# A 16x512x1024 tanh-gated double matmul: the first row tile of x loaded in one transfer

## The chip, the cores and the metric

The kernel runs on one NeuronCore of a Trainium2 chip. Five engines work side by side, each through its own list of instructions in order: TensorE (PE in the profile; its weight loads are listed as PEld), VectorE (DVE), ScalarE (ACT), GpSimd (POOL) and SyncE (SP). SP and ACT start plain DMA transfers, POOL starts DMA transfers that convert float32 to float16 on the way. The metric is the device time of one launch in microseconds; three runs of the kernel before took 296.96, 297.32 and 301.93 us, so the median is 297.32 us.

## The reference

```python
batch, m, k, n = 16, 512, 1024, 768
x: (16, 512, 1024) float32;  w1, w2: (1024, 768) float32

y1 = np.matmul(x, w1)
y2 = np.matmul(x, w2)
return (np.tanh(y1) * y2).astype(np.float32)
```

With batch and rows taken together, x has 8192 rows: 64 row tiles of 128 rows. One row tile is 128x1024 float32, 512 KB; its half along k (512 columns) is 256 KB.

## The kernel before, in words

**Tiling.** The columns of both weight matrices are cut into three blocks: `a` (the first 512 columns of w1), `b` (the first 512 of w2) and `g` (the last 256 of w1 beside the last 256 of w2). Along k there are eight slices of 128. The first four row tiles (0 to 3, `HEAD`) are multiplied plainly: per tile and block eight matmuls of 128x512 are summed in one PSUM bank (line 430), then ACT takes the tanh and DVE multiplies. The other 60 row tiles go in 20 triples. A triple would need 18 products of half a row tile's depth, and is worked out from 15 products (line 457, four matmuls each) of sums of x halves (made by DVE, line 421) and sums of weight blocks (line 412), which ACT and DVE add up (lines 461 and 467), before the tanh (470) and the last multiplication (475).

**Order.** `Planner` orders all the work while the program is built. It knows each operation's cost, what it needs, and when a transfer lands (the table `lands`, and `LANDING` for the transposed tiles), and it writes one order per engine; the 15 products of each triple follow in a fixed order from a start time, `START`. No loop is left at run time. The plan decides which engine does the work where two can, the order on each engine, and the PSUM bank.

**How a row tile gets into place.** Plain matmuls need x transposed in float16. For tiles 0 to 3, SP loads float32 halves: `x00` is tile 0, half 0, `x01` is tile 0, half 1, and so on. Halves `x00` and `x10` are transposed on PE in float32 (`FP32`), the other halves are first converted by DVE (`cx..`, line 368) and then transposed on PE in float16 (`PT..`, line 380). ACT or DVE copies the transposed half from PSUM to SBUF (`e..`, line 366). Only then can the matmuls with that half run.

**Queues at the start.** SP starts its transfers in the order of `on_sp`: first x00, x10, x20, x30, then x01, x60, x11, a4, a5, and so on. ACT starts a0 to a3, the first four k slices of block a, at the same time. The semaphores of these transfers go round a ring of eight, so that SP's fifth transfer waits until one of the first eight has landed, the sixth waits for the next, and so on. The twelve transfers of POOL (block b, and the tiles 4, 5 and the second half of 6) wait behind a small copy that reads a converted g slice (line 504).

**Constant matmuls.** Before any data is there, PE runs the matmuls of `WARM` on a tile of constants, seven of 512 columns into banks 0 to 6 (line 337); their results are not used. After the transposes of x00, and again after those of x10, stands one `FILL`: three more of them, 512, 512 and 256 columns. In the plan the first FILL is free to start after `PT00` and the second after `PT10`.

The calls of the head in the order of the plan before: WARM, PT00, FILL, the first matmul of tile 0 (named m0a0 below: tile, block, k slice), PT10, FILL, m0a1, m1a0, m1a1, PT20, m0a2, m1a2, m2a0, PT30 and so on.

Of the kernel before, what the change touches and what calls it, by code (L numbers as in the profile page):

```python
# [226 lines left out]
def kernel(  # L227
# [21 lines left out]
    XT_BUFS, XH_BUFS, S_BUFS, O_BUFS, C_BUFS = 12, 8, 2, 9, 2  # L249
    WARM = 512, 512, 512, 512, 512, 512, 512  # L250
    FILL = 512, 512, 256
    FREE = 3
    TURNS = (2, 0, 1), (0, 2, 1)
    LANDING = {7: 35.9, 9: 37.2, 8: 39.4, 10: 47.4, 11: 48.3, 12: 49.2, 13: 55.0, 14: 56.3, 15: 57.6}
    rows = list(range(HEAD)) + [HEAD + 3 * i + r for i in range(TRIPLES) for r in (TURNS[i] if i < len(TURNS) else (0, 1, 2))]
# [87 lines left out]
    def x_staged(mt, h):  # L343
        return x_first[mt][:, half(h)] if mt < HEAD else arena[:, STAGED * F:(STAGED + 1) * F]

    def load_first(e, mt, h):
        pin(nc.sync.dma_start(x_staged(mt, h), xf[mt][:, half(h)]))

# [160 lines left out]
    FINE = (5, 36, 37, 45)  # L509
    START = 28.6  # L510
    P7 = 13.0
    ORIGIN = START - 6 * SLOT

# [15 lines left out]
    LAG_FROM, LAG = 21.5, 1.2  # L529
    on_sp = "x00 x10 x20 x30 x01 x60 x11 a4 a5 x21 a6 x31 a7".split() + [f"g{k}{t}" for k in range(KH) for t in range(2)]  # L530
    by_pool = "b0 b4 b1 b5 x61 x4 b2 x51 x50 b6 b3 b7".split()
    GATES = {"b0": ("cg0", w_cols("g", 0)[:, :1])}
    arrivals = on_sp[4:] + by_pool
    size = {"x": 0.68, "a": 0.68, "g": 0.75, "b": 0.63}
    lands = dict(zip("x00 a0 x10 a1 x20 a2 x30 a3".split(), (4.31, 4.47, 6.13, 6.53, 7.7, 8.17, 9.05, 9.44)))
    now = 9.2
    for n in arrivals:
        now += 1.25 if n in by_pool and n[0] == "x" and len(n) == 2 else size[n[0]]
        lands[n] = now + (LAG if now > LAG_FROM else 0.0)

    for k in range(4):
        op(f"La{k}", {"act": 0.45}, -100, [], load_w, "a", k, issued=[f"La{k - 1}"] if k else [], lands=lands[f"a{k}"])
    for n, what in enumerate(on_sp):
        before = [f"L{on_sp[n - 1]}"] if n else []
        if what[0] == "x":
            op(f"L{what}", {"sp": 0.05}, 0.1 * n - 100, [], load_first, int(what[1]), int(what[2]), issued=before, lands=lands[what])
        else:
# [44 lines left out]

    for n, after in enumerate(("PT00", "PT10")):
        op(f"f{n}warm", {"pe": 0.54}, -50, [after], fill, ("f", n), chains=[("f", n)])
    for mt in range(HEAD):
        for h in range(2):
            if (mt, h) not in FP32:
                op(f"cx{mt}{h}", {"dve": 0.37}, lands[f"x{mt}{h}"] - 1, [f"Lx{mt}{h}"], cast_x, mt, h)
            by_pe(mt, h, lands[f"x{mt}{h}"] - 2, f"Lx{mt}{h}" if (mt, h) in FP32 else f"cx{mt}{h}")
        op(f"D{mt}", {"act": 1.05}, START + 8, [f"Lx{mt}0", f"Lx{mt}1"], abs_x, mt, hold=11 + 4 * mt)  # L600
    for mt in rows[HEAD:BY_PE]:
# [154 lines left out]
    for mt in range(MT):  # L756
        i = (mt - HEAD) // 3 if mt >= HEAD else -1
        if mt < HEAD:
            kept = mt == HEAD - 1
            for t in range(2 if mt == 1 else 0):  # L760
                op(f"st{mt}{'ag'[t]}", {"sp": 0.05}, 1e3, outs[mt][t:t + 1], store, mt, t * F, (F, G)[t], behind=[f"p12.{11 + 2 * mt}"], xfer=0.5)
            if mt != 1:
                op(f"st{mt}", {"sp": 0.05}, 1e3, outs[mt][:1] if kept else outs[mt], store, mt, F if kept else 0, G if kept else N, behind=[f"p12.{11 + 2 * mt}"], xfer=1.0)
            for t in range(2 if kept else 0):
                op(f"st{mt}{chr(88 + t)}", {"sp": 0.4, "act": 0.4}, 2e4, outs[mt][1 + t:2 + t], store, mt, t * G, G, xfer=0.4)
            continue
# [37 lines left out]
    for n, cols in enumerate(WARM):  # L804
        constants(banks[n], cols)
    for n in sorted(soon, key=lambda n: plan.start_of[n]):
# [109 lines left out]
```

## Time and profile before

| What | us |
|---|---|
| median of three runs | 297.32 |
| the profiled execution, whole | 297.16 |
| its span on the core, which the profile shows | 295.6 |
| PE busy | 289.5 |
| DVE busy | 255.8 |
| ACT busy | 224.4 |
| POOL busy | 42.3 |

The span begins with the first instruction of the kernel's body and ends with the last one; 1.56 us of the profiled execution lie outside it. "Busy" is the time in which at least one instruction of the engine runs; matmuls are pipelined, so that their starts tell more than their durations. In a row of the timeline the first number is the start in us from the span's start, the second the duration, then come engine, line, operation and tile, the count of instructions that the row merges, and in brackets the idle time before it with what ended it. In a row of the windows stand, for a stretch of time, each engine's busy time with its count of instructions, the granted clock of TensorE, the share of time in which the 16 DMA engines were busy, and the bytes that they moved in GB/s.

### The profile page before, as it was taken

To read this page: it belongs to the slowest core of one execution; us is meant where nothing else is said; L and a number is where in the kernel's file an instruction comes from. 1 tells how busy PE (TensorE), PEld (TensorE's weight loads), DVE (VectorE), ACT (ScalarE), POOL (GpSimd) and SP (SyncE) were. 2 spreads that over 40 slices of the span, in tenths; PEclk is the share of its full clock that TensorE was granted. 3 is DMA by queue.
4 is the path that set the end of the run, shared out by engine and by line. 5 is a ranking of instruction groups with operands and counts; after the bars stand their busy time and mean duration, and the time that the engine had idled before them with its cause. 6 is when DMAs were issued, how large, how long until landed. Compare 5 with 4: busy or idle time off the path is not lost. (4 is left out here: it accounts for less than half of the span.)

```text
span 295.6 us, 4588 instructions
## 1 busy us (share of the span) xinstructions
PE 289.5 (98%) x1374; PEld 132.3 (45%) x1374; DVE 255.8 (87%) x552; ACT 224.4 (76%) x454; POOL 42.3 (14%) x94
## 2 busy tenths in 40 slices
PE   7999999999999999999999999999999999999994
PEld 3445444444444444444444444444444444444442
DVE  1679999999989998898989888898988889898875
ACT  2698599799878878877888888677777767778442
POOL 0065022202102102202012021020211100000000
PEclk9999999999999999999999999999999999999999
DMA  6999999999999999989999999999999999241234
GB/s 217 391 321 204 182 141 169 210 247 230 240 194 197 247 226 216 252 218 239 204 190 246 231 236 270 164 271 264 224 298 225 213 175 324 104 162 53 109 136 169
DMA packets 84858, 63.63 MB, mean 215 GB/s; under 512 B 62816, under 2 KB 67168, under 8 KB 84832
## 3 DMA queue, kind: packets, MB, share of 16 engines
q1 hardware_dynamic: 73888, 45.10, 59.7%
q0 software_dynamic: 9936, 16.65, 36.0%
q10 hardware_dynamic: 1008, 1.57, 1.5%
q8 instruction: 11, 0.18, 0.2%
q14 instruction: 15, 0.12, 0.1%
HBM read 39.85 MB, written 25.17 MB: 220 GB/s over the span
## 5 line engine op out<-in xcount | busy, mean ns | idle before, releaser
L457 PE MATMUL bank<-b,early_x 128*128 128x512 f16 x640 | 148.3, 379 | 0.0
L457 PEld LDWEIGHTS <-early_x 128*128 128x128 f16 x800 | 78.1, 98 | 94.3 <-DVE early_x L421 0.3
L467 DVE TENSOR_TENSOR bank<-bank,arena 128x512 f32<-128x512 f32 x100 | 69.6, 696 | 13.6 <-ACT arena L461 10.9
L461 ACT ACTIVATE arena<-bank 128x512 f32<-128x512 f32 x100 | 57.6, 596 | 18.1 <-PE bank L457 18.1
L475 DVE TENSOR_TENSOR o<-o,bank 128x256 f32<-128x256 f32 (+1 forms) x128 | 61.9, 516 | 7.3 <-ACT o L470 5.9
L390 ACT ACTIVATE junk<-xh 128x1024 f16<-128x1024 f16 x60 | 63.4, 1057 | 0.1
L457 PEld LDWEIGHTS <-xT 128*128 128x128 f16 x400 | 39.0, 98 | 46.9 <-issue 0.4
L457 PE MATMUL bank<-b,xT 128*128 128x512 f16 x240 | 58.3, 379 | 0.0
L470 ACT ACTIVATE o<-bank 128x256 f32<-128x256 f32 (+1 forms) x80 | 34.8, 438 | 26.0 <-DVE bank L467 22.8
L457 PE MATMUL bank<-wh,xT 128*128 128x512 f16 x160 | 41.0, 379 | 0.0
L457 PE MATMUL bank<-wh,early_x 128*128 128x512 f16 x160 | 40.9, 379 | 0.0
L362 POOL DMA_DIRECT2D xh<-in_x_dram x61 | 32.4, 540 | 16.6 <-ACT junk L390 8.6
L421 DVE TENSOR_TENSOR early_x<-early_x,xT 128x512 f16<-128x512 f16 x80 | 33.5, 420 | 0.5
L470 ACT ACTIVATE o<-arena 128x512 f32<-128x512 f32 x40 | 25.2, 629 | 7.5 <-DVE arena L467 7.5
L501 POOL CAST held<-xT 128x1 f32<-128x1 f16 x18 | 4.5, 251 | 161.3 <-DMA xT<-xh 161.3
L461 ACT ACTIVATE bank<-bank 128x512 f32<-128x512 f32 x40 | 21.4, 570 | 4.7 <-PE bank L457 3.9
L430 PE MATMUL bank<-wh,xT 128*128 128x512 f16 x72 | 19.5, 379 | 0.3
L467 DVE TENSOR_TENSOR arena<-bank,arena 128x512 f32<-128x512 f32 x20 | 13.7, 686 | 3.6 <-ACT arena L461 3.6
L421 DVE TENSOR_TENSOR early_x<-xT,xT 128x512 f16<-128x512 f16 x40 | 16.7, 418 | 0.0
L421 DVE TENSOR_TENSOR early_x<-xT,early_x 128x512 f16<-128x512 f16 x40 | 16.7, 418 | 0.0
L467 DVE TENSOR_TENSOR bank<-arena,bank 128x512 f32<-128x512 f32 x20 | 13.8, 692 | 0.1
L390 ACT ACTIVATE junk<-wh 128x768 f16<-128x768 f16 x16 | 13.6, 847 | 0.1
(51 smaller groups left out, 140.0 us busy)
## 6 DMA issues: line engine op xcount, KB each, us to landing
out_dram<-o SPq DMA_DIRECT2D x59, 384.0 KB, 5.1
xh<-in_x_dram POOLq DMA_DIRECT2D x58, 256.0 KB, 6.7
arena<-in_w_dram SPq DMA_DIRECT2D x12, 256.0 KB, 5.6
early_x<-in_x_dram SPq DMA_DIRECT2D x8, 256.0 KB, 4.9
arena<-in_w_dram ACTq DMA_DIRECT2D x4, 256.0 KB, 5.9
wh<-in_w_dram POOLq DMA_DIRECT2D x8, 128.0 KB, 5.5
xT<-xh SPq DMA_TRANSPOSE x57, 4.2
out_dram<-o SPq DMA_DIRECT2D x3, 256.0 KB, 2.5
```

The source lines that it names most:

```text
L362: pin(nc.gpsimd.dma_start(xh(mt)[:, cols], xf[mt][:, cols]))
L390: pin(nc.scalar.activation(junk[:, :src.shape[-1]], src, ACT.Abs, scale=scale, accum_out=sums[:, column:column + 1]))
L421: pin(engine[e].tensor_tensor(x_operand(i, v), x_operand(i, a), x_operand(i, b), OP[how]))
L430: pin(nc.tensor.matmul(bank(chain)[:, :rhs.shape[-1]], xt(mt)[:, k, :], rhs, start=first, stop=k == KO - 1, skip_group_check=True))
L457: pin(nc.tensor.matmul(place(i, dst), x_operand(i, a)[:, k, :], w_rhs(b, k), start=begins and k == 0, stop=k == KH - 1, skip_group_check=T ...
L461: pin(nc.scalar.activation(place(i, dst), place(i, src), ACT.Copy, scale=float(sign)))
L467: pin(nc.vector.tensor_tensor(place(i, dst), a, b, ALU.add if signs == (1, 1) else ALU.subtract))
L470: pin(nc.scalar.activation(out_tile(HEAD + 3 * i + r)[:, lo:lo + n], place(i, src)[:, :n], ACT.Tanh, scale=float(sign)))
L475: pin(nc.vector.tensor_tensor(o, o, place(i, src)[:, at:at + n], ALU.mult))
L501: pin(nc.gpsimd.tensor_copy(held, xt(mt)[:, 0, :1]))
```

## The change

- SP's first transfer is the whole of row tile 0 (`x0`: 128 rows of 4096 bytes, 512 KB) in place of `x00` (128 pieces of 2048 bytes); `x01`, which was SP's fifth transfer, is gone. What needed x00 or x01 now needs x0.
- `WARM` has nine constant matmuls of 512 columns and one of 128 in place of seven of 512; the last two go to banks 0 and 1 again. Of the two FILLs only the one after `PT10` is left.
- The tables of the planner are changed: landing times, `START` and `P7` by 0.5 less, `LANDING` by 0.5 less. The plan is made anew: the order on PE becomes WARM, PT00, PT01, PT10, m0a0, FILL, m0a1, m1a0, PT20, m1a1, m0a2, m1a2, m2a0, PT30. The conversion of x01 is now DVE's first work on data, ahead of that of a0, and DVE instead of ACT copies the second half of tile 0 out of PSUM, ACT instead of DVE that of tile 3. Up to about the sixth triple some operations on DVE and ACT stand in another order and in other banks; from there on the order is the same, with the banks exchanged.
- The result of tile 0 is stored in two transfers (512 and 256 columns) as that of tile 1 was already, in place of one of 768 columns.

```diff
-    WARM = 512, 512, 512, 512, 512, 512, 512
+    WARM = 512, 512, 512, 512, 512, 512, 512, 512, 512, 128
...
-    LANDING = {7: 35.9, 9: 37.2, 8: 39.4, 10: 47.4, 11: 48.3, 12: 49.2, 13: 55.0, 14: 56.3, 15: 57.6}
+    LANDING = {7: 35.4, 9: 36.7, 8: 38.9, 10: 46.9, 11: 47.8, 12: 48.7, 13: 54.5, 14: 55.8, 15: 57.1}
...
     def load_first(e, mt, h):
-        pin(nc.sync.dma_start(x_staged(mt, h), xf[mt][:, half(h)]))
+        if h is None:
+            pin(nc.sync.dma_start(x_first[mt], xf[mt]))
+        else:
+            pin(nc.sync.dma_start(x_staged(mt, h), xf[mt][:, half(h)]))
...
-    START = 28.6
-    P7 = 13.0
+    START = 28.1
+    P7 = 12.5
...
-    on_sp = "x00 x10 x20 x30 x01 x60 x11 a4 a5 x21 a6 x31 a7".split() + [f"g{k}{t}" for k in range(KH) for t in range(2)]
+    on_sp = "x0 x10 x20 x30 x60 x11 a4 a5 x21 a6 x31 a7".split() + [f"g{k}{t}" for k in range(KH) for t in range(2)]
...
-    lands = dict(zip("x00 a0 x10 a1 x20 a2 x30 a3".split(), (4.31, 4.47, 6.13, 6.53, 7.7, 8.17, 9.05, 9.44)))
-    now = 9.2
+    lands = dict(zip("x0 a0 x10 a1 x20 a2 x30 a3".split(), (5.1, 5.1, 6.3, 6.4, 7.5, 7.8, 8.8, 9.1)))
+    now = 8.9
...
+    lands["x00"] = lands["x01"] = lands["x0"]
...
-    for n, after in enumerate(("PT00", "PT10")):
-        op(f"f{n}warm", {"pe": 0.54}, -50, [after], fill, ("f", n), chains=[("f", n)])
+    def x_load(mt, h):
+        return f"Lx{mt}" if f"x{mt}" in on_sp else f"Lx{mt}{h}"
+
+    op("fwarm", {"pe": 0.54}, -50, ["PT10"], fill, ("f", 0), chains=[("f", 0)])
...
-            for t in range(2 if mt == 1 else 0):
+            for t in range(2 if mt < 2 else 0):
...
-            if mt != 1:
+            if mt > 1:
...
-        constants(banks[n], cols)
+        constants(banks[n % len(banks)], cols)
```

More of the change, by code (lines that the diff above doesn't have):

```diff
@@ L545 @@
         if what[0] == "x":
-            op(f"L{what}", {"sp": 0.05}, 0.1 * n - 100, [], load_first, int(what[1]), int(what[2]), issued=before, lands=lands[what])
+            op(f"L{what}", {"sp": 0.05}, 0.1 * n - 100, [], load_first, int(what[1]), int(what[2]) if what[2:] else None, issued=before, lands=lands[what])
         else:
@@ L597 @@
             if (mt, h) not in FP32:
-                op(f"cx{mt}{h}", {"dve": 0.37}, lands[f"x{mt}{h}"] - 1, [f"Lx{mt}{h}"], cast_x, mt, h)
-            by_pe(mt, h, lands[f"x{mt}{h}"] - 2, f"Lx{mt}{h}" if (mt, h) in FP32 else f"cx{mt}{h}")
-        op(f"D{mt}", {"act": 1.05}, START + 8, [f"Lx{mt}0", f"Lx{mt}1"], abs_x, mt, hold=11 + 4 * mt)
+                op(f"cx{mt}{h}", {"dve": 0.37}, lands[f"x{mt}{h}"] - 1, [x_load(mt, h)], cast_x, mt, h)
+            by_pe(mt, h, lands[f"x{mt}{h}"] - 2, x_load(mt, h) if (mt, h) in FP32 else f"cx{mt}{h}")
+        op(f"D{mt}", {"act": 1.05}, START + 8, sorted({x_load(mt, h) for h in range(2)}), abs_x, mt, hold=11 + 4 * mt)
     for mt in rows[HEAD:BY_PE]:
```

## The prediction

> **What bounds the kernel now.** I read the page first: how much of the span TensorE is busy, and where it is not.
>
> ```profile
> span 295.6 us, 4588 instructions
> PE 289.5 (98%) x1374; PEld 132.3 (45%) x1374; DVE 255.8 (87%) x552; ACT 224.4 (76%) x454; POOL 42.3 (14%) x94
> PE   7999999999999999999999999999999999999994
> L467 DVE TENSOR_TENSOR bank<-bank,arena 128x512 f32<-128x512 f32 x100 | 69.6, 696 | 13.6 <-ACT arena L461 10.9
> ```
>
> PE is busy from its first slice to its last one. Whether it is also at its peak is told by the windows (PE's busy time and count are the first two numbers) and by who PE waits for.
>
> ```profile
> 30.00:60.00 30.00, 30.00 (x141) 13.50 (x139) 29.23 (x66) 25.25 (x50) 5.65 (x12) 1.00 1.01 174
> 150.00:180.00 30.00, 30.00 (x141) 13.58 (x140) 26.27 (x56) 24.74 (x54) 3.56 (x8) 1.00 1.06 232
> PEld L457 <- DVE early_x L421: 0.3, 1, 0.3
> PEld L457 <- DVE bank L467: 0.2, 1, 0.2
> ```
>
> 141 matmuls in 30 us are 0.213 us each, in the stretch where DVE is busy 29.23 of 30 us as in the one where it is not. In the list of waits, PE's weight loads wait for DVE once for 0.3 us and once for 0.2 us (the last number is the longest); so the triples stream without a gap. The time is then that of PE's fixed work, plus what PE loses before the stream is dense, plus the tail. The change touches only the head. So I read the timeline of the first 11 us, PE and PEld first.
>
> ```profile
> 1.30 3.17 PE L337 MATMUL bank<-ones 128*128 128x512 bf16 x7 [1.30 <-DVE ones L803]
> 2.13 0.15 PEld L337 LDWEIGHTS <-ones 128*128 128x128 bf16 x1 [0.28 <-issue]
> 2.55 0.15 PEld L337 LDWEIGHTS <-ones 128*128 128x128 bf16 x1 [0.28 <-issue]
> 4.67 0.98 PE L380 MATMUL bank<-ident,early_x 128*128 128x128 f32 x4 [0.21 <-DMA early_x<-in_x_dram]
> 5.49 0.71 PE L337 MATMUL bank<-ones 128*128 128x512 bf16 x3
> 6.33 0.10 PEld L430 LDWEIGHTS <-xT 128*128 128x128 f16 x1 [0.52 <-ACT xT L366]
> 6.56 0.60 PE L380 MATMUL bank<-ident,early_x 128*128 128x128 f32 x4
> 6.99 0.71 PE L337 MATMUL bank<-ones 128*128 128x512 bf16 x3
> 7.54 0.90 PE L430 MATMUL bank<-wh,xT 128*128 128x512 f16 x3
> 8.47 0.40 PE L380 MATMUL bank<-ident_h,xh 128*128 128x128 f16 x4
> 8.82 1.12 PE L430 MATMUL bank<-wh,xT 128*128 128x512 f16 x3
> 9.54 0.10 PEld L430 LDWEIGHTS <-xT 128*128 128x128 f16 x1 [0.62 <-ACT xT L366]
> 10.70 0.39 PE L380 MATMUL bank<-ident_h,xh 128*128 128x128 f16 x4
> 10.92 0.38 PE L430 MATMUL bank<-wh,xT_kept 128*128 128x512 f16 x1
> 7.19 0.59 ACT L366 CAST xT<-bank 128x512 f16<-128x512 f32 x1 [0.92 <-PE bank L380]
> 7.98 0.43 DVE L368 CAST xh<-early_x 128x512 f16<-128x512 f32 x1 [0.74 <-DMA early_x<-in_x_dram]
> ```
>
> The reader is to see a chain of arrivals: PT00 at 4.67 waited for a DMA, m0a0 at 6.33 for ACT's copy, PT20 at 8.47 for DVE's conversion, which itself waited for x20 until 7.98, and m2a0 (the weight load at 9.54) for ACT's copy of PT20. Around 9.54 the waits end. So I compare the kernels by **when m2a0 runs and what has run by then**.
>
> How fast the data come is in the windows of one us (the last two numbers are the DMA engines' busy share and GB/s):
>
> ```profile
> 2.00:3.00 1.00, 1.00 (x4) 0.31 (x3) 0.00 (x0) 0.12 (x1) 0.00 (x0) 1.00 0.81 195
> 3.00:4.00 1.00, 1.00 (x4) 0.27 (x2) 0.00 (x0) 1.00 (x1) 0.00 (x0) 1.00 0.95 315
> 4.00:5.00 1.00, 0.79 (x4) 0.36 (x3) 0.27 (x1) 0.16 (x1) 0.00 (x0) 1.00 0.76 238
> 5.00:6.00 1.00, 1.00 (x7) 0.68 (x5) 0.16 (x1) 0.31 (x1) 0.00 (x0) 1.00 0.87 291
> 6.00:7.00 1.00, 0.87 (x8) 0.66 (x7) 0.18 (x1) 0.28 (x1) 0.00 (x0) 1.00 1.05 404
> ```
>
> From 6 us on the DMA engines are full at 404 GB/s. Before that there is a ramp, and a hole from 4 to 6 us (0.76 and 0.87 busy) that opens when the first transfers are in.
>
> **The change part by part.** The sum is made against the profiled execution's own time, 297.16 us (295.6 of span and 1.56 around it); the median of the runs, 297.32, is 0.16 above it.
>
> *The front.* The constant matmuls start 0.42 us apart (2.13, 2.55), the clock's slow half: PT00's four take 0.82 us to the next start (4.67 to 5.49), PT10's four 0.43 (6.56 to 6.99). Nine at 0.425 and a quarter of one, from 1.30, end at 5.24. Until then PE can do nothing else. What hides it is the wait for x0. x0 and a0 are 786 kB; the windows have moved 748 by 5.0 and 786 by 5.13. The 524 kB of x00 and a0 were through at 4.06, and PT00 came 0.61 later; with the same lag PT00 comes at 5.74, at best at 5.24. PT01 follows at most 0.65 later (DVE's conversion 0.43, its own 0.22), by 6.39. As PT10 is later than that in every case below, front and x0 cost nothing; without that cover they would cost up to 0.5 us.
>
> *One FILL less, PT01 earlier.* A FILL is 0.55 us (6.99 to 7.54). The removed one lay in the wait of m0a0 for ACT, so that its removal alone gives nothing; it gives what the new order can put there, which is PT01, 0.22 us (10.70 to 10.92) that need not be done later.
>
> *The chain behind PT10.* With PT10 at P: its 0.43, m0a0 0.21, FILL 0.55, m0a1 and m1a0 0.21 each, so PT20 not before P+1.61; m1a0's copy by ACT is there at P+1.27 (6.56, then 7.19 + 0.59 and 0.05). From PT20 to m2a0 it is 1.07 (8.47 to 9.54), from the start of x20's conversion to PT20 0.49 (7.98 to 8.47). So m2a0 comes at the later of P+2.68 and C+1.56, C being the start of that conversion.
>
> *What comes when.* x01 used to be SP's fifth transfer and is now inside the first: 262 kB more stand ahead of x10 and x20, 0.65 us at 404 GB/s. Against it stands what the larger first transfer recovers of the early idle DMA time; call that **r**. So P = 7.21 - r, C = 8.63 - r, and m2a0 = 10.19 - r by the second term (9.89 - r by the first). Before, m2a0 ran at 9.54 without PT01; the gain is 9.54 + 0.22 - 10.19 + r = **r - 0.43**.
>
> *r, from both sides.* Below: 0, the engines being idle for another reason than too few bytes queued. Above: the whole shortfall from 2 to 6 us, (808 - 510) + (808 - 529) = 577 kB or 1.43 us. I take the hole from 4 to 6 alone, 279 kB or 0.69 us, since it lies just behind the first transfers, where each engine would now have twice the bytes from SP; the ramp before it has the start in it, which nothing moves. Gain: **0.26 us**.
>
> The Trainium skill speaks against this part: "DMA: Bandwidth & Descriptors", section "Why small descriptors are slow (HBM only)", gives each packet a fixed cost of about three bus cycles beside 32 bytes a cycle, so that 4096-byte rows in place of 2048-byte ones spare about 2% of x0, by an estimate from that page 0.03 us. By that rule r is near 0 and the sum is that of the slower rival below. That the DMA engines reach 404 GB/s with 2048-byte rows agrees with it; that they were idle between 4 and 6 us is not something it speaks of.
>
> *After the head* the loads set the pace once more, with no slack at all:
>
> ```profile
> 17.68 0.44 POOL L504 CAST held<-wh 128x1 f32<-128x1 f16 x1 [16.13 <-DVE wh L368]
> 20.28 1.09 POOL L362 DMA_DIRECT2D xh<-in_x_dram  x2
> 27.24 0.45 PEld L380 LDWEIGHTS <-xh 128*128 128x128 f16 x8 [0.36 <-DMA xh<-in_x_dram]
> 28.49 0.29 PEld L380 LDWEIGHTS <-xh 128*128 128x128 f16 x4 [0.25 <-DMA xh<-in_x_dram]
> ```
>
> The transposes at 27.24 and 28.49 start when POOL's loads land. The bytes that go before those loads are the same in total, and POOL's first load waits for a converted g slice, itself one of SP's loads; so they come r = 0.69 earlier, more than the 0.26 that PE wants. I take no loss here.
>
> *Exchanges and order.* One copy out of PSUM goes from ACT to DVE, another back: net nothing. The new order of DVE and ACT in the first six triples has the same operations; PE's two waits for DVE (0.3 and 0.2) say how little it depends on it. Bounds 0 and one addition late, 0.70 us (the page's row of line 467); I take 0.
>
> *The store of tile 0 in two.* One more issue on SP, among these, in the middle of a run:
>
> ```profile
> 148.40 1.05 SPq L427 DMA_DIRECT2D out_dram<-o  x2
> 153.43 2.16 SPq L387 DMA_TRANSPOSE xT<-xh  x1
> ```
>
> Two issues take 1.05 us, so one is 0.53; behind it SP is free from 149.45 to 153.43. Nothing; without that cover the next transpose starts 0.53 later.
>
> **Sum:** 297.16 - 0.26 = 296.90 us.
>
> **The rivals.** *x01 in the way (slower).* With r = 0, x20's conversion starts at 8.63 and m2a0 runs at 10.19: 0.43 us lost, 297.59. For it: the 0.65 us are certain bytes, r is not, and m0a0, which ran at 6.33, now stands behind PT10. Against it: the hole. It decides at r = 0.43: less recovered than that, and the kernel is slower.
>
> *Hidden anyway.* The head gains, but POOL's loads land at the old times, because their spacing is set by POOL's queue and not by the bytes ahead. Then PE stands at 27.24 as before: 297.16. For it: those two waits without slack; against it: the gate at 17.68 moves with the g loads.
>
> *The whole ramp goes.* r = 1.43: x20's conversion at 7.20, m2a0 at 8.76, gain 1.00, 296.16. Against it: the first us has nothing to do with sizes.
>
> *The clock falls back.* With a FILL less, PE stands idle between PT01 and PT10, 0.1 to 0.8 us; if that put the clock back to half for another 4 us, as at the start (1.30 to 5.49), some 10 matmuls would cost 0.21 more each, 2.1 us, 299.3. Against it: PE stood idle ahead of PT00 at 4.67 and was at full speed at 5.49. The Trainium skill, "TensorE: Matmul & The Clock Gate", Part 1, asks for an idle window of about 3.4 us before the clock falls; by that rule this case is out.
>
> **How the numbers follow.** Forecast (0.1 to 0.8 faster) 0.48; hidden anyway, within 0.1: 0.20; x01 in the way 0.24; whole ramp 0.06; the clock or a later stall 0.02. The predicted time is the forecast's, 296.9. The range goes from the whole ramp, 296.16, to the slower rival, 297.59, widened by 0.3 at its upper end because the runs before lie 0.36 apart between the lowest and the median: 296.2 to 297.9. A change of 2%, about what a measurement of this kernel can tell from no change, is 5.9 us; no case reaches it, so faster 0.01, same 0.97, slower 0.02.
>
> **What would show it.** PT00 between 5.24 and 5.74; PT10 near 6.5; x20's conversion near 7.9; m2a0 near 9.5 with PT01 done; 4 to 6 us at about 400 GB/s; the first wait for x4 near 26.8; PE's last matmul 0.26 earlier than before. It is wrong if the hole stays (then x20 is late and the kernel slower), if the wait at 27.24 stays where it is, or if DVE gets into PE's way between 30 and 100 us.

## The result, and the profile after

| | kernel before | changed kernel |
|---|---|---|
| median of 22 runs each, on the same chip | 297.25 us | 298.91 us |
| lowest of them | 296.82 us | 297.94 us |
| profiled execution, whole / span | 297.16 / 295.6 us | 298.26 / 296.7 us |

The ratio is 1.0048, 95% interval 1.0032 to 1.0065: no change by the measure of 2%, but clearly slower, by 1.0 to 1.9 us. The forecast was 296.9 us with a range from 296.2 to 297.9; the time lies above the range, and on the other side of the kernel before. (The slowest executions, some 302 us and more, which either kernel has, are not in the ratios.)

From the page of the changed kernel:

```profile
span 296.7 us, 4583 instructions
PE 289.5 (98%) x1374; PEld 131.9 (44%) x1374; DVE 255.9 (86%) x552; ACT 224.5 (76%) x454; POOL 43.4 (15%) x94
```

PE's work is the same to a tenth of a microsecond (289.5); the 1.1 us more of span are time in which PE waited, but for 0.1 us behind its last matmul. To see how much, I compare when PE's last eight matmuls start in each kernel (first line: before; second: changed).

```profile
290.29 1.04 PE L430 MATMUL bank<-wh,xT_kept 128*128 128x256 f16 x8
```

```profile
291.30 1.04 PE L433 MATMUL bank<-wh,xT_kept 128*128 128x256 f16 x8
```

They start 1.01 us later. Below, "PE behind" is this difference for each kernel.

**The head** went nearly as the sum said. Timeline of the changed kernel (PE, PEld and DVE):

```profile
5.09 0.62 PE L383 MATMUL bank<-ident,early_x 128*128 128x128 f32 x4
5.55 0.39 PE L383 MATMUL bank<-ident_h,xh 128*128 128x128 f16 x4
6.75 0.66 PE L383 MATMUL bank<-ident,early_x 128*128 128x128 f32 x4 [0.81 <-DMA early_x<-in_x_dram]
8.16 0.43 DVE L371 CAST xh<-early_x 128x512 f16<-128x512 f32 x1 [0.70 <-DMA early_x<-in_x_dram]
8.64 0.23 PEld L383 LDWEIGHTS <-xh 128*128 128x128 f16 x4 [0.47 <-DVE xh L371]
9.72 0.10 PEld L433 LDWEIGHTS <-xT 128*128 128x128 f16 x1 [0.24 <-ACT xT L369]
```

PT00, PT01, PT10, the conversion of x20, PT20 and the weights of m2a0: P = 6.75, C = 8.16, m2a0 at 9.72. Before, m2a0's weights came at 9.54 without PT01; with PT01's 0.22 already done, the head is 0.04 us ahead. Everything else is lost behind 9.72.

**How fast the data came.** Windows of the changed kernel, last two numbers DMA share and GB/s:

```profile
3.00:4.00 1.00, 1.00 (x4) 0.43 (x3) 0.00 (x0) 1.00 (x1) 0.00 (x0) 1.00 1.00 389
4.00:5.00 1.00, 1.00 (x4) 0.30 (x2) 0.03 (x1) 0.23 (x1) 0.00 (x0) 1.00 0.99 336
5.00:6.00 1.00, 0.94 (x10) 0.70 (x8) 0.76 (x3) 0.25 (x1) 0.00 (x0) 1.00 0.97 299
13.00:14.00 1.00, 1.00 (x10) 0.49 (x8) 0.76 (x2) 0.89 (x3) 0.00 (x0) 1.00 0.99 323
14.00:15.00 1.00, 0.98 (x5) 0.24 (x3) 0.41 (x2) 0.72 (x2) 0.00 (x0) 1.00 0.96 302
```

and of the kernel before, in the same two stretches from 13 us on (its rows up to 7 us stand in the prediction):

```profile
13.00:14.00 1.00, 1.00 (x7) 0.39 (x4) 0.73 (x2) 1.00 (x3) 0.00 (x0) 1.00 1.06 391
14.00:15.00 1.00, 1.00 (x9) 0.51 (x7) 0.52 (x2) 0.98 (x4) 0.00 (x0) 1.00 1.04 373
```

The hole of 4 to 6 us is partly filled (336 and 299 GB/s for 238 and 291). But between 13 and 15 us the changed kernel moves 139 kB less (323 and 302 for 391 and 373), 0.34 us at 404 GB/s: most of what was won is given back. This is no accident of one profile, and it goes with the load. From 13 to 15.5 us all thirteen traces with x0 in one transfer show 315 to 363 GB/s, whatever their plan and constant matmuls, and all seven without it 367 to 379.

**Where PE waits now.** Timeline of the changed kernel, weight loads, POOL and ACT:

```profile
15.17 0.23 PEld L383 LDWEIGHTS <-xh 128*128 128x128 f16 x4 [0.50 <-DVE xh L371]
17.89 0.44 POOL L507 CAST held<-wh 128x1 f32<-128x1 f16 x1 [16.35 <-DVE wh L371]
20.06 0.74 PEld L433 LDWEIGHTS <-xT 128*128 128x128 f16 x4 [0.35 <-issue]
27.28 0.39 PEld L383 LDWEIGHTS <-xh 128*128 128x128 f16 x5 [0.21 <-DMA xh<-in_x_dram]
27.94 0.21 PEld L383 LDWEIGHTS <-xh 128*128 128x128 f16 x3 [0.27 <-issue]
26.24 1.08 ACT L393 ACTIVATE junk<-early_x 128x1024 f16<-128x1024 f32 x1
27.28 1.66 ACT L369 COPY xT<-bank 128x512 f16<-128x512 f16 x3
```

First place, 14 to 20 us: a transpose (15.17, of x31) stands in PE's order ahead of other matmuls, and it waits for a conversion that came late by the plan. x31 landed at 14.66, earlier than in the kernel before (14.89); but the new table promised it at 13.66 (8.9 and seven transfers of 0.68), a full microsecond too early, where the old one promised 14.64. Between PE's starts at 14.6, 17.6 and 19.6 stand 0.36, 0.10 and 0.24 us more than the matmuls need; in the kernel before it was 0.09, 0.11 and 0.05 in this stretch. Second place, 27.4 us: PT40 is out at 27.40, and PT41 waits until 27.93; its bank still holds PT61, whose copy (27.28) stands behind ACT's sum of absolute values (26.24). By 33 us PE is 0.67 us behind. Third place, 90 us (DVE, ACT, PE):

```profile
89.22 0.42 DVE L478 TENSOR_TENSOR o<-o,bank 128x256 f32<-128x256 f32 x1
89.55 0.69 DVE L470 TENSOR_TENSOR bank<-arena,bank 128x512 f32<-128x512 f32 x1
90.28 0.38 ACT L473 ACTIVATE o<-bank 128x256 f32<-128x256 f32 x1
90.72 1.02 PE L460 MATMUL bank<-wh,xT 128*128 128x512 f16 x4 [0.18 <-ACT o L473]
```

A multiplication that was put off (89.22) is taken ahead of the addition (89.55) on which tanh (90.28) waits; the bank that tanh frees is PE's next one. That is 0.35 us more between PE's starts than the matmuls need. From there to the end PE stays 1.01 us behind.

### The profile page after: what moved, and what is told of

Same layout as the page of the kernel before. It is cut to its first block, busy times and chain, and to the rows that moved or that the text cites. A ratio compares the mean times of both kernels' runs of the same rounds, so it can differ in the third digit from the quotient of the medians.

```text
span 296.7 us, 4583 instructions
## 1 busy us (share of the span) xinstructions
PE 289.5 (98%) x1374; PEld 131.9 (44%) x1374; DVE 255.9 (86%) x552; ACT 224.5 (76%) x454; POOL 43.4 (15%) x94
## 5 line engine op out<-in xcount | busy, mean ns | idle before, releaser
L504 POOL CAST held<-xT 128x1 f32<-128x1 f16 x18 | 5.6, 312 | 168.3 <-DMA xT<-xh 168.3
```

Source lines behind the costliest of these rows:

```text
L504: pin(nc.gpsimd.tensor_copy(held, xt(mt)[:, 0, :1]))
```

## The experiments

"PE behind" is the start of PE's last eight matmuls against 290.29 in each profile, so it belongs to one execution, and the median to all; the last column is the longest way from issue to landing among the last seven stores.

| kernel | median us (runs) | ratio, 95% interval | profiled us | PE behind | last stores |
|---|---|---|---|---|---|
| e1_after_again | 298.25 (7) | 1.0038, 1.0022 to 1.0055 | 298.08 | 0.66 | 2.65 |
| e2_later | 297.98 (12) | 1.0025, 1.0015 to 1.0035 | 297.85 | 0.48 | 2.68 |
| e3_warm | 297.45 (12) | 1.0019, 1.0004 to 1.0034 | 297.08 | -0.02 | 2.19 |
| e4_before_again | 297.10 (1) | | 297.10 | 0.01 | 2.29 |
| e5_abs_first | 297.58 (12) | 1.0011, 1.0002 to 1.0020 | 297.78 | 0.54 | 2.45 |
| e6_old_plan | 299.02 (6) | 1.0064, 1.0047 to 1.0080 | 297.45 | -0.16 | 3.61 |
| e7_two_halves | 298.34 (4) | 1.0041, 1.0026 to 1.0055 | 298.10 | 0.22 | 2.99 |
| e8_plan_alone | 297.84 (10) | 1.0024, 1.0015 to 1.0033 | 298.26 | 1.23 | 2.20 |
| e9_old_plan_again | 301.51 (1) | | 301.51 | 3.90 | 3.57 |
| e10_old_plan_fill | 298.47 (12) | 1.0020, 0.9993 to 1.0046 | 297.25 | -0.12 | 2.20 |
| e11_changed_fill | 298.69 (12) | 1.0012, 0.9978 to 1.0046 | 299.53 | 2.00 | 2.78 |
| e12_old_plan_third | 299.79 (1) | | 299.79 | 0.38 | 4.27 |
| e13_load_alone | 298.89 (12) | 1.0045, 1.0019 to 1.0072 | 299.63 | 1.02 | 3.71 |
| e14_warm_alone | 297.98 (12) | 1.0017, 0.9991 to 1.0043 | 297.62 | 0.39 | 2.37 |
| e15_split_alone | 297.63 (12) | 1.0003, 0.9981 to 1.0026 | 297.52 | -0.02 | 2.50 |
| e16_fill_no_split | 298.40 (12) | 1.0025, 0.9996 to 1.0055 | 298.51 | 1.02 | 2.20 |
| e17_true_table | 298.71 (12) | 1.0040, 1.0025 to 1.0055 | 297.56 | 0.45 | 3.17 |
| e18_load_alone_again | 298.17 (1) | | 298.17 | -0.42 | 3.71 |

### Repeats, and the postponed multiplications

The changed kernel and the kernel before as they are (e1, e4), and the changed kernel with the hold of the postponed multiplications moved by the same 0.5 us as its `START`:

```diff
-    LATER = {mt: 66.0 + 13.0 * mt for mt in range(HEAD - 1)}
+    LATER = {mt: 65.5 + 13.0 * mt for mt in range(HEAD - 1)}
```

> The changed kernel once more, for a second profile. Theory: it is slower than the kernel before by a ratio of 1.003 to 1.0065, for two reasons that must both show again: products of the triples run 0.4 to 0.9 us later than before from 33 us on (late loads in the head), and one more stall of about 0.35 us near 90 us, ahead of a product whose bank ACT frees late. Rival: the DMA engines' slack rate between 13 and 15.5 us (302 to 323 GB/s in the first profile against 385 or more before) was an accident of that execution; then the rate there is 380 or more now, and the delay from 33 us on is under 0.3 us.

> The kernel before once more, for a second profile. Theory: the loads land within 0.15 us of the first profile's times up to 15 us (x10 at 6.37, x20 at 7.96), and the rate between 13 and 15.5 us is 380 GB/s or more. Rival: the landing times scatter by 0.3 us or more between executions; then differences of that size between the two kernels' profiles say nothing.

> The changed kernel with the hold of the three postponed multiplications of tiles 0 to 2 (LATER) moved by the same 0.5 as the plan's start; from the 59th operation on, DVE's order is then that of the kernel before. Theory: the stall of 0.35 us near 90 us is DVE's order (a 256-column multiplication ahead of an addition), so it goes, and the kernel is 0.3 to 0.4 us faster than the changed one, ratio to before about 1.003. Rival: the stall comes from the exchanged banks or from that one execution; then the ratio stays that of the changed kernel, 1.0048.

The repeats put PE 0.66 and 0.01 us behind: the loss is no accident of one execution. The rate from 13 to 15.5 us is low again in e1 (338 GB/s, after 315) and high again in e4 (379, after 376), so e1's rival falls; but the lag at 33 us, 0.32, is less than the 0.4 to 0.9 of its theory. In e4 x10 and x20 land within 0.13 us of the first profile (6.36 and 8.09). When x4 lands, the two profiles of the kernel before are 0.32 apart (27.20 and 26.88), and so are those of the changed kernel (27.24 and 26.92); single profiles can't tell smaller differences there. In e2_later the addition stands ahead of the multiplications again, and PE goes through 90 us without a wait:

```profile
88.56 0.70 DVE L470 TENSOR_TENSOR bank<-arena,bank 128x512 f32<-128x512 f32 x1
89.17 1.41 DVE L478 TENSOR_TENSOR o<-o,bank 128x256 f32<-128x256 f32 x4
90.19 1.03 PE L460 MATMUL bank<-wh,xT 128*128 128x512 f16 x4
```

So the third place (0.34 in e1, 0.35 in the first profile, none in e2) comes from one absolute time that was left unmoved when the start was moved. The intervals of e1 and e2 overlap; the profile is what tells them apart, and the ratio, 1.0025, is close to the 1.003 that I expected.

### The sums of absolute values

e2_later with one more edit:

```diff
-        op(f"D{mt}", {"act": 1.05}, START + 8, sorted({x_load(mt, h) for h in range(2)}), abs_x, mt, hold=11 + 4 * mt)
+        op(f"D{mt}", {"act": 1.05}, START + 8, sorted({x_load(mt, h) for h in range(2)}), abs_x, mt, hold=10.0 + 4 * mt)
```

> The changed kernel with the multiplications' hold moved with the start (as in e2_later), and the sums of absolute values of tiles 0 to 3 held only until 10 + 4*mt instead of 11 + 4*mt, so that ACT has done them before the copy that frees tile 6's second bank. Theory that the order written by the plan costs the time: the wait of 0.2 to 0.3 us at about 27.4 us goes, products lie 0.2 to 0.3 us behind those of the kernel before from 33 us on (0.49 in e2_later), ratio 1.001 to 1.002. Rival, that PE is there too early for tile 4's load anyway: the wait is taken over by the load, lag 0.45 to 0.5 us, ratio 1.0025.

The wait at 27.4 is gone: PT40 and PT41 are out in one piece.

```profile
27.47 0.61 PE L383 MATMUL bank<-ident_h,xh 128*128 128x128 f16 x8
```

PE is still 0.54 us behind, since in this execution, one of the longer of its twelve, the first place cost more (0.24 and 0.47 us more between starts at 13.3 and 14.9 than the matmuls need; in e2_later 0.23 and 0.12). The time, 297.58 us and 1.0011, is the nearest to the kernel before of all that keep the changed loads and plan. The mechanism at 27.4 held, and so did the ratio; the lag that I expected in the profile, 0.2 to 0.3, did not.

Taken together, two numbers of the plan took the ratio from 1.0048 (1.0038 in the repeat) to 1.0011, with the new load, the constant matmuls and the stores left as they were. The interval of e5, 1.0002 to 1.0020, lies below those of the changed kernel (from 1.0032 and from 1.0022). So most of the changed kernel's loss goes with two numbers of its plan, and can be taken back without touching the load.

### The plan's numbers alone, and the old plan with the new load

e8: the kernel before, with its loads, and only numbers of the plan set as early as in the change. e6, e9 and e12 are one kernel, the change with the plan's numbers of before and a table near the measured landings.

From the kernel before to e8 (`START`, `P7` and `LANDING` as in the change):

```diff
-    START = 28.6
-    P7 = 13.0
+    START = 28.1
+    P7 = 12.5
...
-    lands = dict(zip("x00 a0 x10 a1 x20 a2 x30 a3".split(), (4.31, 4.47, 6.13, 6.53, 7.7, 8.17, 9.05, 9.44)))
-    now = 9.2
+    lands = dict(zip("x00 a0 x10 a1 x20 a2 x30 a3".split(), (5.1, 5.1, 6.3, 6.4, 7.5, 7.8, 8.8, 9.1)))
+    now = 8.22
```

From the changed kernel to e6, e9 and e12 (`START`, `P7` and `LANDING` back as before):

```diff
-    START = 28.1
-    P7 = 12.5
+    START = 28.6
+    P7 = 13.0
...
-    lands = dict(zip("x0 a0 x10 a1 x20 a2 x30 a3".split(), (5.1, 5.1, 6.3, 6.4, 7.5, 7.8, 8.8, 9.1)))
-    now = 8.9
+    lands = dict(zip("x0 a0 x10 a1 x20 a2 x30 a3".split(), (4.9, 5.0, 6.5, 6.9, 8.0, 8.5, 9.3, 9.9)))
+    now = 9.7
```

> The kernel before with its loads, constant matmuls and stores as they were, and only the plan's numbers and landings set as early as the change sets them (START 28.1, P7 12.5, LANDING 0.5 less, the loads behind the first eight 0.98 earlier in the table). Theory that the too early table costs the time: waits of 0.3 to 0.6 us together at 13 to 15 us and 0.2 to 0.3 at 27.4, products 0.3 to 0.7 us behind from 33 us on, ratio 1.001 to 1.004 although no load is changed. Rival, that the load costs it: lag 0.1 us or less, ratio 0.999 to 1.001.

> The changed loads, constant matmuls and stores, but the plan's numbers (START, P7, LANDING) of the kernel before, and a table of landings close to those measured (x0 4.9, x10 6.5, x20 8.0, x30 9.3, the rest from 9.7 on). Theory that the plan's too early times cost the time, not the load: the waits at 13 to 15 us shrink to 0.2 us or less together, none at 27.4 and 90 us, products lie 0.0 to 0.15 us behind from 33 us on, ratio 1.000 to 1.002. Rival, that the whole-row load and the slower transfers at 13 to 15 us cost it: lag 0.3 to 0.5 us whatever the order, ratio 1.002 to 1.0035.

> The kernel of e6_old_plan once more, to see an execution of the longer kind: its six executions took 297.45 to 299.93 us, and the profile was that of the shortest. Theory that the clock is at fault: with the constant matmuls behind tile 0's first transpose gone, TensorE idles about 0.6 us ahead of x10, and where the time at which the clock rises falls behind that gap it rises 1 to 3.5 us later; then the record shows 512-column matmuls at 0.43 us from a start instead of 0.21 beyond 7 us, and the products lie 0.8 to 2.5 us behind. Rival, that the transfers vary: the clock is full before 7 us and a wait for a transfer (x20, x30, x4) carries the 0.8 to 2.5 us.

> The kernel of e6_old_plan a third time, for the same question as e9_old_plan_again: clock theory, 512-column matmuls of 0.43 us from start to start beyond 7 us in an execution of 298.4 us or more; rival, full clock before 7 us and a longer wait for a transfer.

e8 has no changed load and loses too: ratio 1.0024, half of the changed kernel's loss. PE is 1.23 us behind, in a profile that is one of the longer of its ten runs, by waits of its own in the same stretch:

```profile
14.22 0.23 PEld L380 LDWEIGHTS <-xh 128*128 128x128 f16 x4 [0.62 <-DVE xh L368]
26.71 0.23 PEld L380 LDWEIGHTS <-xh 128*128 128x128 f16 x4 [0.58 <-DMA xh<-in_x_dram]
```

That rules out that only the load costs: **numbers that promise data too early are enough**. Turned round, e6 has the new load with the old numbers, and PE is 0.16 us ahead of the kernel before, in e9 0.28 ahead until 160 us. In these two executions the load wins about what the prediction gave it, on PE, once the order fits it; in e12, the same kernel, PE is 0.38 us behind, by waits between 11 and 16 us.

The time did not follow: e6's ratio, 1.0064, is no better than the changed kernel's, so of its two cases neither holds whole: the waits at 13 to 15, 27.4 and 90 us are gone as the theory said, but the time is longer than either case had it. Its six runs lie between 297.45 (the profiled one) and 299.93, and e9 and e12 show two reasons. In e9 tanh waited for the store that holds its output buffer:

```profile
  ACT o L473: 3.5, 1
DMA to landing us min/median/max: 3.1/5.7/9.6
```

This is from the view of the output tensor between 140 and 175 us: who waited for it, and how long its stores took. They took no longer than in the kernel before (3.5/6.6/9.8 there). The store that tanh waited for was late in starting: at 153.99 us, where the same store started at 148.74 in e6, the same kernel, and at 148.40 in the kernel before. Why SP's queue was so late is not known, and as one of the first three runs of the kernel before took 301.93 us, it need not belong to the change. PE then stood for 2.34 us, and what followed ran at half the granted clock (windows of e9, the clock is the number ahead of the last two):

```profile
162.00:165.00 3.00, 0.96 (x5) 0.33 (x4) 0.26 (x1) 1.38 (x3) 0.00 (x0) 1.00 1.13 328
166.00:169.00 3.00, 3.00 (x9) 1.03 (x7) 2.71 (x7) 2.38 (x6) 1.60 (x3) 0.50 1.30 212
170.00:173.00 3.00, 3.00 (x15) 1.37 (x14) 2.82 (x7) 2.39 (x6) 0.00 (x0) 1.00 1.05 277
```

The Trainium skill, "TensorE: Matmul & The Clock Gate", section "Why this matters for your kernels", asks to keep PE's gaps under about 3 us. Here the clock fell with a gap of 2.34 us, shorter than that, in the one case that the traces hold; the measurement decides. In e12 PE is 0.38 behind and the last stores land late. The clock theory of these two, a late rise in the head, is wrong for both: the clock was full by 5.2 us in both. The rival, varying transfers, is nearer to what they show; but it named waits for loads, and these are mainly stores.

### A table that tells the truth, with the new plan

e5_abs_first with the table of e6; `START`, `P7` and `LANDING` stay those of the change.

> As e5_abs_first (the changed kernel's own plan, with the multiplications' hold moved and the sums of absolute values earlier), but with a table of landings close to those measured (x0 4.9, x10 6.5, x20 8.0, x30 9.3, the rest from 9.7 on). If the too early table is what is left of the loss: the waits at 13 to 15 us (0.24 and 0.47 in e5_abs_first) fall to 0.2 us or less together, products 0.2 us behind the kernel before or level with it, ratio 0.999 to 1.001, and the kernel is no slower than the one before. If the new order of the triples brings waits of its own, or the transfers decide: products 0.4 us or more behind, ratio 1.001 to 1.004.

The ratio is 1.0040 and PE 0.45 us behind. The waits at 13 to 15 us are gone (none over 0.05 us between starts), and at 20 us PE is 0.13 us ahead of the kernel before. But then PE waits for loads at 25.8 and 27.1 (0.21 and 0.15), and it has a new wait of 0.25 at 41.4. The rival holds: the planner's order shifts as a whole with each number, and a truer table alone does not give back the time. No version here beats the kernel before.

### The load by itself

e7: e2_later, with tile 0 in two half-row transfers, both at the head. e13 and e18 are one kernel: of the change only the load, with the table near the measured landings; WARM, FILLs, stores and the plan's numbers are those of before.

For e7:

```diff
-    on_sp = "x0 x10 x20 x30 x60 x11 a4 a5 x21 a6 x31 a7".split() + [f"g{k}{t}" for k in range(KH) for t in range(2)]
+    on_sp = "x00 x01 x10 x20 x30 x60 x11 a4 a5 x21 a6 x31 a7".split() + [f"g{k}{t}" for k in range(KH) for t in range(2)]
...
-    arrivals = on_sp[4:] + by_pool
+    arrivals = on_sp[5:] + by_pool
...
-    soon = {"L" + n for n in on_sp[:4]} | {f"La{k}" for k in range(4)}
+    soon = {"L" + n for n in on_sp[:5]} | {f"La{k}" for k in range(4)}
```

For e13 and e18, from e6 (and the store of tile 0 in one):

```diff
-    WARM = 512, 512, 512, 512, 512, 512, 512, 512, 512, 128
+    WARM = 512, 512, 512, 512, 512, 512, 512
...
-    op("fwarm", {"pe": 0.54}, -50, ["PT10"], fill, ("f", 0), chains=[("f", 0)])
+    for n, after in enumerate(("PT00", "PT10")):
+        op(f"f{n}warm", {"pe": 0.54}, -50, [after], fill, ("f", n), chains=[("f", n)])
```

> As e2_later, but tile 0 comes as two transfers of half rows, one behind the other at the head of the queue, instead of one of whole rows. If the length of the rows filled the hole of 4 to 6 us: the hole comes back (about 250 GB/s or less in 4 to 5 us, 336 in the changed kernel) and x20's transfer lands 0.3 to 0.6 us later than the 8.1 of the changed kernel, the products 0.3 us or more behind e2_later's. If it was only that the second half was moved ahead and stands in the hole: rates of 3 to 6 us as in the changed kernel, x10 and x20 within 0.15 us of it, ratio as e2_later's 1.0025.

> Of the change only the load of tile 0 in whole rows at the head of the queue; constant matmuls, stores and the plan's numbers (START, P7, LANDING) are those of the kernel before, the table of landings is close to those measured. Theory that the load itself gains what the prediction said (0.1 to 0.3 us) and the plan's numbers lose it: products 0.1 to 0.3 us ahead of the kernel before from 33 us on, shortest executions 296.7 to 297.0 us. Theory that the executions spread because of the load: most of them 298.3 us or more as in e6_old_plan, ratio 1.003 or more. Theory that they spread because of the constant matmuls or the split store: they gather at 296.7 to 297.3 us, ratio 0.999 to 1.0.

> The kernel of e13_load_alone once more. If the idle time of about 0.7 us between the last constant matmul and x0 puts off the rise of the clock: full clock again only at 6.5 us or later (8.94 in e13_load_alone, 4.2 to 6.2 in kernels whose front lasts until x0), products 0.5 to 1.1 us behind. If the late rise of e13_load_alone was chance: full clock before 6 us and products 0.1 to 0.3 us ahead.

Windows of e7:

```profile
3.00:4.00 1.00, 1.00 (x4) 0.43 (x3) 0.00 (x0) 1.00 (x1) 0.00 (x0) 1.00 0.89 287
4.00:5.00 1.00, 1.00 (x4) 0.30 (x2) 0.00 (x0) 0.15 (x1) 0.00 (x0) 1.00 1.06 408
5.00:6.00 1.00, 0.87 (x6) 0.52 (x4) 0.09 (x1) 0.09 (x1) 0.00 (x0) 1.00 1.04 391
14.00:15.00 1.00, 1.00 (x9) 0.46 (x8) 0.76 (x2) 0.83 (x3) 0.00 (x0) 1.00 1.04 357
```

and its PT10 in the timeline:

```profile
7.37 0.66 PE L383 MATMUL bank<-ident,early_x 128*128 128x128 f32 x4 [0.58 <-DMA early_x<-in_x_dram]
```

The hole is filled with short rows too (408 and 391 GB/s), and at 14 to 15 us the rate is 357 for the changed kernel's 302. So it is not the length of the rows that fills it, but that there is something to move. Neither of my two expectations held whole: the hole stays filled, yet x10 lands at 7.33 in place of 6.71 and PT10 comes at 7.37 in place of 6.75. I take the cause to be that x10 now stands behind two transfers and what ACT starts beside them; that was not tried. The ratio 1.0041 is worse than e2_later's although PE is only 0.22 behind; its last stores are slow as well.

e13 and e18 are the same kernel, and their heads differ by the clock (e13, then e18). The rise of the clock is read here from the starts of the matmuls and from the trace's list of clock changes; ahead of the first change the windows print 1.00, also where the constant matmuls start 0.42 us apart.

```profile
7.07 0.63 PE L383 MATMUL bank<-ident_h,xh 128*128 128x128 f16 x4
7.92 1.06 PE L383 MATMUL bank<-ident,early_x 128*128 128x128 f32 x4
8.77 0.80 PE L337 MATMUL bank<-ones 128*128 128x512 bf16 x3
```

```profile
6.72 0.66 PE L383 MATMUL bank<-ident,early_x 128*128 128x128 f32 x4
7.22 0.71 PE L337 MATMUL bank<-ones 128*128 128x512 bf16 x3
```

PT10's four matmuls take 0.85 us to the next start in e13 and 0.50 in e18: in e13 the clock was still at half until about 8.9 us, and PE lost 1.02 us; in e18 it was full by 5 us, and PE is 0.42 us ahead, the best of all. So of e18's two cases that of chance holds: a gap in front of x0 (0.66 us in e13, 0.54 in e18) may go with a late rise, and need not. Nor does a late rise need the gap: in kernels whose front lasts until x0 the clock was full only at 7.33 (e1), 6.69 (e2), 7.17 (e5) and 7.08 (e14), later than the 4.2 to 6.2 that I had given for them. All twelve runs of e13 lie at 298.3 us or more, ratio 1.0045: that is the case of its expectation in which the load spreads the executions. But e2 and e5 have the load too, with one run of twelve each at 298.3 or more, so the load does not do it everywhere. e18, with PE 0.42 ahead, still took 298.17: there the rest is lost behind PE's last matmul.

### The constant matmuls

e3: the kernel before with the changed WARM (its banks as in the change) and only the second FILL. e14: the same WARM, both FILLs. e10 and e11: e6_old_plan and the changed kernel with the first FILL back, behind PT01.

For e3 and e14, from the kernel before; the lines behind the "..." for e3 alone:

```diff
-    WARM = 512, 512, 512, 512, 512, 512, 512
+    WARM = 512, 512, 512, 512, 512, 512, 512, 512, 512, 128
...
-    for n, after in enumerate(("PT00", "PT10")):
-        op(f"f{n}warm", {"pe": 0.54}, -50, [after], fill, ("f", n), chains=[("f", n)])
+    op("fwarm", {"pe": 0.54}, -50, ["PT10"], fill, ("f", 0), chains=[("f", 0)])
```

For e10 and e11:

```diff
-    op("fwarm", {"pe": 0.54}, -50, ["PT10"], fill, ("f", 0), chains=[("f", 0)])
+    for n, after in enumerate(("PT01", "PT10")):
+        op(f"f{n}warm", {"pe": 0.54}, -50, [after], fill, ("f", n), chains=[("f", n)])
```

> The kernel before with the changed constant matmuls alone: nine and a quarter in front, no FILL behind the transposes of x00. Theory: no change, ratio 1.000 within 0.0007: the transposes of x00 start 0.57 us later, at 5.24, those of x10 0.2 us later, and those of x20 wait for their load at 8.47 as before. Rival: the front's half us goes through to the end, 0.2 to 0.5 us slower, ratio 1.001 to 1.002.

> The kernel before with the longer constant matmuls in front (9 of 512 columns and one of 128) and with both fills kept. If the constant matmuls spread the executions (five of twelve above 298.3 us in e3_warm): the same here, ratio 1.001 to 1.003. If not: 297.0 to 297.4 us, ratio 0.999 to 1.001.

> As e6_old_plan, with the three constant matmuls (512, 512, 256 columns) put back, now behind PT01, where TensorE would idle. Theory of the clock: the executions gather within 0.5 us, at 296.9 to 297.4 us, ratio 0.999 to 1.001 (the products of e6_old_plan's profile were 0.16 us ahead). Rival, that transfers or something else spread the executions: 298 to 299.5 us as without the fill, ratio 1.003 to 1.006.

> The changed kernel with the three constant matmuls put back behind PT01. Theory of the clock: the executions above 298.5 us (11 of 22 of the changed kernel) go; what is left is the plan's order, 0.65 to 1.0 us behind, so 297.9 to 298.2 us, ratio 1.0025 to 1.0035. Rival, that all of the loss is the order's: 298.3 to 298.9 us, ratio 1.004 to 1.005.

With the old load the longer front ends later than x00 lands; whether that costs PE anything depends on the clock. In e3 it cost nothing on PE (-0.02). In e14 PT00 took 0.86 us to the next start and all three matmuls of the FILL ran slow:

```profile
5.21 1.06 PE L380 MATMUL bank<-ident,early_x 128*128 128x128 f32 x4
6.07 1.21 PE L337 MATMUL bank<-ones 128*128 128x512 bf16 x3
```

and PE stayed 0.39 us behind. The time is another matter. e3's ratio, 1.0019, is above the 1.000 within 0.0007 of its theory and fits its rival, and five of its twelve runs lie at 298.3 us or more. So do five of twelve of e14, as it was to be if the constant matmuls spread the executions; its interval reaches below 1. On the same chips the kernel before had 2 of 24 and 3 of 35 runs there. So the longer front spreads the executions even with the old load; by what, no trace shows.

e10 and e11 did not gather: twelve runs from 297.25 to 302.55 and from 297.92 to 304.96, seven and nine of them at 298.3 us or more, where the kernel before had 5 of 23 on that chip, with a median of 297.37. The clock theory of the spread falls with them. Their intervals reach below and above 1, so they decide nothing on the FILL.

### The split store, and the late last stores

e15: the kernel before with tile 0's store in two. e16: e10_old_plan_fill with it in one.

```diff
-            for t in range(2 if mt == 1 else 0):
+            for t in range(2 if mt < 2 else 0):
...
-            if mt != 1:
+            if mt > 1:
```

> The kernel before with tile 0's store in two parts and nothing else. If the split costs nothing: ratio 0.999 to 1.001, executions at 297.0 to 297.4 us. If one more store in the queue makes later stores late: some executions with a wait of tanh for a store at 140 to 165 us, or late last stores, 298 us and more, ratio 1.002 to 1.005.

> As e10_old_plan_fill (old plan's numbers, whole-row load, longer constant matmuls, fill behind PT01), with tile 0's store in one part. If the split store spread the executions there (297.25 to 300.1 us): they gather at 296.9 to 297.5 us, ratio 0.998 to 1.000. If it is the load or the disturbance of the transfers in itself: seven of twelve or so stay above 298.3 us, ratio 1.002 to 1.004.

The split alone leaves PE where it was (-0.02), ratio 1.0003, 0.9981 to 1.0026. Its runs lie at 297.28 to 298.58 us, median 297.63 for 297.27 of the kernel before on that chip, a little above the 297.0 to 297.4 that I expected; so a cost of a few tenths is not ruled out. e16 without the split spreads as e10 did, 297.18 to 300.5 us. So it is not the split that spreads those executions. In e16's profile PE waited 0.65 us for a cast of a g slice that was itself waiting for its transfer:

```profile
23.48 1.76 PE L433 MATMUL bank<-wh,xT 128*128 128x512 f16 x6 [0.65 <-ACT wh L369]
```

What the late ends have in common is seen in the DMA view of the last microseconds. The kernel before, 284 to 288 us, and its last stores; then e18, 292 to 295, and its last stores:

```profile
q8 instruction: 1, 0.02, 1.9%
...
out_dram<-o SPq DMA_DIRECT2D x3, 128.0 KB, 2.3
```

```profile
q8 instruction: 1, 0.02, 1.8%
...
out_dram<-o SPq DMA_DIRECT2D x3, 128.0 KB, 3.7
```

The queue of instruction transfers has one packet of 16 KB every 22 to 36 us. In fourteen of the twenty traces the last of them starts 4.3 to 4.6 us before PE's last matmul and no store at the end takes over 3.0 us. In the other six (e6, e9, e12, e13, e17, e18) it starts between 1.9 us before PE's last matmul and 2.4 us after it, among the last stores, and three or more of them take 2.9 to 4.3 us. In e12, e13 and e18, where it starts after PE's last matmul, the end comes 5.9 to 6.8 us behind PE's last matmul, in place of 4.6 in the kernel before. That the transfer causes the delay is argued from its falling together, not tried; nor is it known why it comes late in these kernels.

## Why the prediction was wrong

- **The front** and **one FILL less**: right for PE in the profile. PT00 at 5.09 (I gave 5.24 to 5.74; the front itself ended a little earlier, the clock having risen before its end), PT01 at 5.55, hidden by the wait for x10. That the longer front spreads the executions (e3, e14) the prediction had no term for.
- **The chain behind PT10**: right to the hundredth. m2a0 came at C + 1.56 = 8.16 + 1.56 = 9.72.
- **r**: the mechanism held in part, and the size was off. The slower rival's r = 0 is out. From x20's conversion r = 8.63 - 8.16 = 0.47, from PT10 7.21 - 6.75 = 0.46, where I took 0.69. The hole of 4 to 6 us filled by 106 kB out of 279; as much came between 2 and 4 us (225 and 389 GB/s for 195 and 315), in the ramp that I had said nothing moves. The gain of the head is 0.04, not 0.26, hard by the point r = 0.43 from which the slower rival decides. With 0.04 us less of r the head would have lost, and half of r came from elsewhere than I had said: that the sign of this term came out right is luck. By this correction alone the time would have been 297.12.
- **"After the head ... I take no loss"**: wrong. POOL's loads did not come r earlier: their gate opens at 17.89 in place of 17.68, with the transfers of 13 to 15 us slower; tile 4 is waited for at 27.28 as at 27.24 before. That is the time that the rival "hidden anyway" gave them, though not for its reason, POOL's own spacing; PE's own waits come on top.
- **"Exchanges and order ... I take 0"**: the step that failed most. I counted operations and found them the same; but PE takes its work in the order written, and the order was written for landings that did not come true (x31 promised at 13.66, landed at 14.66). It has the three places of waits (0.4 more than before, 0.32 and 0.35 us in the first profile). e8 shows that the plan's numbers alone cost half of the ratio, without any change of load; e2 and e5 show that the waits at 90 and at 27.4 go with one number each, and with them most of the ratio (1.0048 to 1.0011). My upper bound, one addition late or 0.70 us, was less than what was lost (1.05 from m2a0 on). And the two waits of PE for DVE in the kernel before said how well *that* order fitted, not how little PE depends on the order.
- **The store in two**: right on PE (e15), within the 0.2% that its interval leaves open.
- **The clock falls back**: not in the changed kernel. In both its profiles the clock rises once (4.93 and 7.33 us) and stays full to the last matmul. In e9 it fell with a wait of 2.34 us, so the mechanism is real where the wait is long. My argument against it was none: in the kernel before the clock rose only at 5.42 us, so that the idle time ahead of PT00 at 4.67 could not have put it back.
- **The range** had its upper end at the rival's 297.59 and 0.3; the only case with a loss behind the head, "the clock or a later stall", had a chance of 0.02. Of the three signs of being wrong that it named, two came: the wait at 27.24 stayed, and DVE got into PE's way at 90 us. Open is why the executions spread more than those of the kernel before, so that the median, 298.91, is 0.65 above the profiled 298.26. It goes with no single part: with the new load e2 and e5 have one run of twelve each at 298.3 us or more and e13 all twelve, and with the old load e3 and e14 have five of twelve. Open is also why the load alone, with the old numbers, is slower in time (e13, 1.0045) though PE can be ahead with it.

## What to carry to other kernels

Where one order per engine is written out beforehand, a table of expected landings is part of the kernel: a change that moves times in it is priced by what each in-order engine will now wait for, not by counting operations, and every absolute time in the plan has to move together. Bytes won early in a stream of transfers are worth something only if the wait that ends last, further on, is for the same stream and gets them; look at the rate until that wait. An engine that finishes earlier is not a kernel that finishes earlier: look at what comes after its last instruction too.

## What the runs showed of the hardware that I had not expected

- By the traces' lists of clock changes, the clock rose to full at other times in executions of one and the same kernel: at 4.38 us in e18 and 8.94 in e13, at 4.93 in the first profile of the changed kernel and 7.33 in e1. PE was 0.42 us ahead in e18 and 1.02 behind in e13.
- A gap of 2.34 us on PE, from 163.0 to 165.3 us, was followed by half the clock from 165.6 to 169.0 us (e9).
- With x0 in one transfer the DMA rate from 13 to 15.5 us was 315 to 363 GB/s in all thirteen traces, with the engines 0.95 to 1.05 busy; without it 367 to 379 in all seven. One of these is e7, which has the same bytes in two half-row transfers at the head: 371. The cause is not known.
- An instruction transfer of 16 KB among the last stores went with stores of 2.9 to 4.3 us in place of 2.0 to 3.0.
